# One core of a decoder layer: a gated mixer computed with tokens on the partitions instead of channels

## The chip, the cores and the metric

The kernel runs on one core of a Trainium2 chip. The time is that of one execution on the device, in microseconds. A core has five engines that run side by side, each working through its own list of instructions in order: TensorE (PE, with its weight loads shown apart as PEld), VectorE (DVE), ScalarE (ACT), GpSimd (POOL) and SyncE (SP), which starts transfers. They wait for one another by semaphores. TensorE's clock has two levels, 1.2 and 2.4 GHz.

## The reference

A layer takes 1088 tokens (1024 of a prompt and 8 x 8 of samples) with 1024 channels. After an RMS norm one projection makes three parts of 512 columns. The first goes to an S5 state-space mixer. The other two, u and v, go to the chunk mixer, which this case is about:

```python
def chunk_mixer(uv, ln_g, ln_b, w_s, b_s):
    uv = jax.nn.gelu(uv)
    u = uv[..., :CM_WIDTH]                              # CM_WIDTH 512
    v = layernorm(uv[..., CM_WIDTH:], ln_g, ln_b)
    ...
    vc = vp.reshape(Bn, n_chunks, Lc, CM_HEADS, CM_HEAD_DIM)   # 8 heads of 64, chunks of 128
    w = jnp.where(mask[None], w_s[:, :Lc, :Lc], jnp.zeros((), w_s.dtype))
    mixed = jnp.einsum('hts,bcshd->bcthd', w, vc)
    mixed = mixed + jnp.transpose(b_s[:, :Lc])[None, None, :, :, None]
    out = u * mixed
    return out, v[:, start:]

mix = jnp.concatenate([rmsnorm(o_s5, g_s5[l]), rmsnorm(o_cm, g_cm[l])], axis=-1)
x = x + mix @ w_out[l]
```

Behind it a gated feed-forward block (FFN) and a last norm follow.

## The kernel before

**Numbers.** A product of 32-bit numbers is made of three faster ones: each operand is split into a high and a low part (`split`: ScalarE copies the high part, L146, VectorE subtracts it, L147), and `mm3` issues three matmuls (L150 to L152). Small products (the spatial mixes, S5's own, transposes) are done on unsplit 32-bit operands; the trace shows such a matmul as two records, except for transposes.

**Layout.** xh and xl hold the split activations, features on the partitions: eight blocks of 128 features by 1088 tokens. The tokens stand in three pieces c of 384, 384 and 320 columns, or in nine tiles j of 128 (tile 8 takes the last 128 columns, of which the upper 64 are the samples). v is kept with tokens on the partitions, 128 x 9 x 512.

**Order.** One list of Python code is given to a scheduler, which simulates the engines and writes each engine's instructions in the order that comes out; `tc.issue_after` holds work back to a chosen point. PSUM banks are taken in turn from tags: mm has four, s5 three, sp one.

**Stages.** First the norm and the S5 part of the projection (pu, to us, through memory to U). From 72 us on two things run side by side:
- the S5 chain, eight times s5_a, s5_b, s5_c: four transposes (ptr, L502) of PT (VectorE, L491 to L493, from the transfer bc), matmuls sb (L509), kb (L517), yb (L585, L586), with many steps on VectorE between; its outputs ys go to memory as ys_d, and come back as g.
- the chunk mixer. `v_quarter` makes v (pv, 24 matmuls of N=256 a tile, tokens stationary, then a gelu on ScalarE, L650); `ln` normalizes it (a pow on GpSimd, L657). `cm_out(q, c)`, for q = 4 and 5 (the halves of u) and three pieces c, makes u with features on the partitions (`fm_group`, pu, 48 matmuls of N=384 or 320), scales it on VectorE by rB (the norm's factor, L673) and applies the gelu; then the spatial mix spt (L680): v is the weight, 64 columns for one head, w moves with 128 columns, two heads fill the two column halves of the array. VectorE adds the bias bB and multiplies by u (L691, L692). ScalarE squares, VectorE adds the squares up (sqo, L698). bB contains the row sums of w, which two matmuls rsw (L636) against a matrix of ones make early. `cm_mix(c)` sums the squares over partitions (ss, a matmul with ones, L164), makes the inverse root (`rsqrt_bc`, L171 to L174), scales on VectorE (L718) and splits into rows 4 to 7 of xh and xl.

Then s5_act splits g (L770, L771) into rows 0 to 3 of xh and xl, `glu` runs the pg matmuls (banks of tags mm and s5 in turn), `wo_tile` the output projection po, and the FFN follows.

Of the kernel before, what the change touches and what calls it, by code (L numbers as in the profile page):

```python
# [83 lines left out]
def layer_kernel(ctx: ExitStack, tc: tile.TileContext, A, O, dbg=None):  # L84
# [69 lines left out]
    SQB = {"cw": 1, "prep": SQP}  # L154
# [49 lines left out]
    cwp = Arena("cw", cwf, {"ur": (0, 384, 2), "sq": (768, 384, 1), "rsy": (1152, 384, 1)})  # L204
# [428 lines left out]
    for q in range(2):  # L633
        p = bank("rsw", "sp")
        with tc.issue_after(MM[RG].ins):
            PE.matmul(p, ones, wT[:, 4 * q:4 * q + 4, :].rearrange("p h t -> p (h t)"), start=True, stop=True)  # L636
        for i in range(4):
            m, h = divmod(4 * q + i, 2)
            hs = slice(64 * h, 64 * h + 64)
            V.scalar_tensor_tensor(bB[hs, m, :], p[hs, 128 * i:128 * i + 128], gcol("lnb", m)[hs], bB[hs, m, :],  # L640
                                   op0=ALU.mult, op1=ALU.add)
# [18 lines left out]
    def om_blocks(m, c):  # L660

        if c < 2:
            return [(v[:, 3 * c:3 * c + 3, 128 * m:128 * m + 128], 0, 384)]
        return [(v[:, 6:8, 128 * m:128 * m + 128], 0, 256), (v[:, 8, 128 * m:128 * m + 64], 256, 64)]

    def cm_out(q, c):

        n0, n = CH[c]
        pp = fm_group(q, c)
        for i in range(2):  # L670
            m = 2 * (q - 4) + i
            ur = cwp.tile([128, 384], F32, tag="ur", name="ur", bufs=2)[:, :n]
            V.tensor_tensor(ur, pp[i], rB[:, n0:n0 + n], ALU.mult)  # L673
            S.activation(ur, ur, AF.Gelu_apprx_tanh)
            p = bank("spt", "s5" if (q, c) > (5, 1) else "sp")[:, :n]
            for x in range(0, n, 128):
                j = (n0 + x) // 128
                r0, w = (0, wT) if j < 8 else (64, bd)
                for h in range(2):
                    PE.matmul(p[64 * h:64 * h + 64, x:x + 128 - r0], v[r0:128, j, 128 * m + 64 * h:128 * m + 64 * h + 64],  # L680
                              w[r0:128, 2 * m + h, :], start=True, stop=True)
            for om, o, w in om_blocks(m, c):
                d = [x[:, o:o + w] for x in (p, ur, sqo[:, n0:n0 + n])]
                t_ = 128 if w > 64 else 8
                d = [x.rearrange("p (j t) -> p j t", t=t_) for x in d]
                om = om.rearrange("p (j t) -> p j t", t=t_) if w == 64 else om
                if w > 64:
                    bias = bB[:, m:m + 1, :].to_broadcast([128, w // 128, 128])
                else:
                    bias = bB[:, m, 0:128:16].unsqueeze(2).to_broadcast([128, 8, 8])  # L690
                V.scalar_tensor_tensor(om, d[0], gcol("lng", m), bias, op0=ALU.mult, op1=ALU.add)  # L691
                V.tensor_tensor(om, om, d[1], ALU.mult)  # L692
                if m == 0:
                    S.activation(d[2], om, AF.Square)
                    continue
                sq = tmp_sq(cwp, w, "sq").rearrange("p (j t) -> p j t", t=t_)
                S.activation(sq, om, AF.Square)
                V.tensor_tensor(d[2], d[2], sq, ALU.add)  # L698
# [18 lines left out]
    def scaled_split(src, g, rb, hi, lo):
        V.scalar_tensor_tensor(src, src, g, rb, op0=ALU.mult, op1=ALU.mult)  # L718
        split(src, hi, lo)

    def cm_mix(c):
        n0, n = CH[c]
        rb = rsqrt_bc(cwp, sum_sq(sqo[:, n0:n0 + n], n), n, 1.0 / W)
        for m in range(4):
            for om, o, w in om_blocks(m, c):
# [614 lines left out]
```

## Time and profile before

| | before |
|---|---|
| median of 3 runs | 1105.35 us (1104.3 to 1107.51) |
| the profiled execution, its span | 1104.05 us, 1102.3 us |
| TensorE busy | 1049.9 us, 95% |
| VectorE busy | 852.9 us, 77% |
| ScalarE busy | 434.3 us, 39% |
| GpSimd busy | 320.5 us, 29% |
| mean granted clock of TensorE | .985 of full |

The busy shares are means over the whole span. What a change in one stage is worth is read in that stage, from what is busy and what waits there. The records of a matmul overlap: a matmul of .28 us whose successor starts .12 us later costs .12.

### The profile page before, as it was taken

What the parts mean: (1) busy time and instruction counts of PE and PEld (TensorE: products, weight loads), DVE (VectorE), ACT (ScalarE), POOL (GpSimd) and SP (SyncE); (2) the same over time, 40 slices, a digit from 0 to 9 for tenths busy, and PEclk for the clock granted to TensorE, in tenths of its full rate; (3) what the DMA queues carried; (4) which work ended last, traced back from release to release, by engine and by line L of the source; (5) the groups of instructions that cost most, each with busy time, mean ns of one, the idle gap of its engine ahead of it and who ended that gap; (6) DMA issues with size and microseconds to landing.
All of it is one profiled execution on the core that took longest, in us unless ns stands there. A gap on an engine that the chain in (4) does not pass through costs nothing.

```text
span 1102.3 us, 20323 instructions
## 1 busy us (share of the span) xinstructions
PE 1049.9 (95%) x7966; PEld 1026.8 (93%) x7966; DVE 852.9 (77%) x1724; ACT 434.3 (39%) x812; POOL 320.5 (29%) x287
## 2 busy tenths in 40 slices
PE   7899999979999799999999999999998999999994
PEld 6899998879999699999999999999998999999994
DVE  6987999999998996666666666657668768758886
ACT  7314333487544543233233232233244325314651
POOL 5010350000000435425435334435433333223220
PEclk9989999989999899999999999999999999999998
DMA  8342334375332113223224223133156816514304
GB/s 278 108 129 65 89 99 124 90 225 164 113 113 95 39 58 129 77 90 129 75 76 137 82 77 128 59 110 127 61 181 219 303 40 205 184 35 151 119 16 162
DMA packets 81520, 131.19 MB, mean 119 GB/s; under 512 B 8977, under 2 KB 60049, under 8 KB 81297
## 3 DMA queue, kind: packets, MB, share of 16 engines
q1 hardware_dynamic: 81424, 129.91, 36.3%
q8 instruction: 62, 1.02, 0.4%
q14 instruction: 34, 0.27, 0.1%
HBM read 90.43 MB, written 34.24 MB: 113 GB/s over the span
## 4 chain that ended last, share of the span: by engine, by line
PE 50%; DVE 7%; DMA 5%; issue 2%; ACT 1%; POOL 0%; DVEq 0%; ACTq 0%; POOLq 0%; SPq 0%
PE u L152 12%; PE u L150 12%; PE u L151 12%; DMA h<-hid_d 4%; PE ua L152 3%; PE ua L151 2%; PE ua L150 2%; PE ub L151 1%; PE ub L152 1%; DVE xl L147 1%; PE ub L150 1%; ACT xh L146 1%; DVE fb L147 1%; PE uc L151 1%; PE uc L152 1%
## 5 line engine op out<-in xcount | busy, mean ns | idle before, releaser
L1059 POOL TENSOR_TENSOR tS<-q,q 128x512 f32<-128x512 f32 x22 | 28.6, 1301 | 251.7 <-DVE h L921 146.1
L150 PE MATMUL u<-xh,h 128*128 128x272 f32 x344 | 99.1, 288 | 0.0
L151 PE MATMUL u<-xl,h 128*128 128x272 f32 x344 | 99.0, 288 | 0.0
L152 PE MATMUL u<-xh,h 128*128 128x272 f32 x344 | 98.9, 288 | 0.0
L146 ACT ACTIVATE h<-q 128x512 fp32r<-128x512 f32 (+1 forms) x83 | 50.7, 614 | 81.7 <-PE u L151 56.8
L147 DVE TENSOR_TENSOR h<-q,h 128x512 fp32r<-128x512 f32 (+1 forms) x83 | 72.6, 876 | 4.3 <-ACT h L146 2.5
L150 PE MATMUL pu<-xh,cwr 128*128 128x384 f32 (+1 forms) x192 | 65.5, 345 | 6.2 <-DVE us L303 6.2
L1097 ACT ACTIVATE st<-st 128x272 f32<-128x272 f32 x88 | 37.8, 431 | 72.0 <-DVE st L1119 34.8
L152 PE MATMUL pu<-xh,cwr 128*128 128x384 f32 (+1 forms) x192 | 65.1, 342 | 0.0
L151 PEld LDWEIGHTS u<-xl,h 128*128 128x128 f32 x344 | 64.9, 189 | 0.0
L151 PE MATMUL pu<-xl,cwr 128*128 128x384 f32 (+1 forms) x192 | 64.8, 338 | 0.0
L150 PEld LDWEIGHTS u<-xh,h 128*128 128x128 f32 x344 | 64.7, 188 | 0.0
L152 PEld LDWEIGHTS u<-xh,h 128*128 128x128 f32 x344 | 64.6, 188 | 0.0
L1064 POOL TENSOR_TENSOR tS<-tS,q 128x512 f32<-128x512 f32 x22 | 30.0, 1363 | 111.3 <-DVE h L147 59.6
L146 ACT ACTIVATE fb<-q 128x512 fp32r<-128x512 f32 (+1 forms) x64 | 38.9, 609 | 58.3 <-PE u L151 35.8
L152 PE MATMUL u<-xh,fb 128*128 128x272 f32 x208 | 61.1, 294 | 0.6 <-DVE fb L147 0.6
L150 PE MATMUL u<-xh,fb 128*128 128x272 f32 x208 | 60.6, 291 | 0.1
L151 PE MATMUL u<-xl,fb 128*128 128x272 f32 x208 | 60.5, 291 | 0.0
L147 DVE TENSOR_TENSOR fb<-q,fb 128x512 fp32r<-128x512 f32 (+1 forms) x63 | 53.4, 850 | 5.3 <-ACT fb L146 4.4
L152 PE MATMUL po<-xh,cwr 128*128 128x272 f32 x192 | 55.9, 291 | 0.0
L151 PE MATMUL po<-xl,cwr 128*128 128x272 f32 x192 | 55.8, 290 | 0.0
L150 PE MATMUL po<-xh,cwr 128*128 128x272 f32 x192 | 55.5, 289 | 0.0
(498 smaller groups left out, 4122.8 us busy)
## 6 DMA issues: line engine op xcount, KB each, us to landing
hid_d<-st SPq DMA_DIRECT2D x22, 952.0 KB, 4.2
h<-hid_d SPq DMA_DIRECT2D x28, 544.0 KB, 4.0
q<-in_w_gate_dram SPq DMA_DIRECT2D x22, 512.0 KB, 3.5
q<-in_w_up_dram SPq DMA_DIRECT2D x22, 512.0 KB, 3.5
q<-in_w_d_dram SPq DMA_DIRECT2D x16, 512.0 KB, 3.7
wo<-in_w_out_dram SPq DMA_DIRECT2D x14, 512.0 KB, 4.9
wi<-in_w_in_dram SPq DMA_DIRECT2D x12, 512.0 KB, 5.1
h<-hid_d SPq DMA_DIRECT2D x14, 408.0 KB, 3.1
```

The source lines that it names most:

```text
L146: S.activation(hi, src, AF.Copy)
L147: return (eng or V).tensor_tensor(lo, src, hi.bitcast(F32), ALU.subtract)
L150: PE.matmul(p, wh, ah, start=start, stop=False, **kw)
L151: PE.matmul(p, wh, al, start=False, stop=False, **kw)
L152: return PE.matmul(p, wl, ah, start=False, stop=stop, **kw)
L1059: P.tensor_tensor(tS, a21, a22, ALU.add)
L1064: P.tensor_tensor(tS, tS, a11, ALU.subtract)
L1097: S.activation(dst, src, AF.Silu)
```

## The change

u is now computed with tokens on the partitions, like v: `cm_u(q, j)` issues 24 matmuls of N=256 for a tile, and ScalarE applies the norm's factor (r1c, a column) and the gelu at once. The spatial mix takes w (128 x 128) as the weight and moves 64 columns of v for each of four heads, `cm_out(q, j)`. The bias becomes two tables BT of 128 x 512, made by 16 operations of ScalarE from 16 small matmuls rsw of N=1. VectorE adds and multiplies, 256 wide; ScalarE squares and sums along the row at once (ssc). `cm_mix(j)` works tile by tile: three tiny operations on GpSimd make the factor, ScalarE scales the row, TensorE transposes four blocks into one bank (pt), and for each of them ScalarE writes the high part and VectorE the low part. The three ss sums, rsqrt_bc's and the adding up of squares go, and ln's factor lng is applied within ln. `CL` sets how many tiles cm_out and cm_mix follow cm_u by.

```diff
+CL = 1, 3
-    cwp = Arena("cw", cwf, {"ur": (0, 384, 2), "sq": (768, 384, 1), "rsy": (1152, 384, 1)})
+    cwp = Arena("cw", cwf, {"ur": (0, 256, 2), "bt": (512, 512, 2)})
...
-    for i in range(2):
-        Q.dma_start(bB[64 * i:64 * i + 64], A["bB"][i:i + 1].to_broadcast([64, 4, 128]))
+    Q.dma_start(bsc, A["bB"])
...
-    for q in range(2):
-        p = bank("rsw", "sp")
-        with tc.issue_after(MM[RG].ins):
-            PE.matmul(p, ones, wT[:, 4 * q:4 * q + 4, :].rearrange("p h t -> p (h t)"), start=True, stop=True)
...
+    p = bank("rsw", "sp")
+    with tc.issue_after(MM[RG].ins):
+        for h in range(8):
+            PE.matmul(p[:, h:h + 1], wT[:, h, :], ones[:, 0:1], start=True, stop=True)
+            PE.matmul(p[64:128, 8 + h:9 + h], bd[64:128, h, :], ones[64:128, 0:1], start=True, stop=True)
+    S.activation(rsc[:, 0:8], p[:, 0:8], AF.Copy)
+    S.activation(rsc[64:128, 8:16], p[64:128, 8:16], AF.Copy)
+    BT = []
+    for i in range(2):
+        t, r0 = cwp.tile([128, W], F32, "bt"), 64 * i
+        for h in range(8):
+            hs, i_ = slice(64 * h, 64 * h + 64), 8 * i + h
+            S.activation(t[r0:128, hs], lnb[r0:128, hs], AF.Identity, scale=rsc[r0:128, i_:i_ + 1],
+                         bias=bsc[r0:128, i_:i_ + 1])
+        BT.append(t)
...
-        V.tensor_scalar(mv[:, j, 1:2], mv[:, j, 1:2], EPS, None, op0=ALU.add)
+        P.tensor_scalar(mv[:, j, 1:2], mv[:, j, 1:2], EPS, None, op0=ALU.add)
         P.tensor_tensor(mv[:, j, 1:2], mv[:, j, 1:2], mhalf[:, 0:1], ALU.pow)
-        V.tensor_scalar(vj, vj, mv[:, j, 0:1], mv[:, j, 1:2], op0=ALU.subtract, op1=ALU.mult)
+        V.scalar_tensor_tensor(vj, vj, mv[:, j, 0:1], lng, op0=ALU.subtract, op1=ALU.mult)
+        S.activation(vj, vj, AF.Copy, scale=mv[:, j, 1:2])
+    def cm_u(q, j):
+        p = bank("pv")
+        for k in range(8):
+            wh, wl = wq(q, k, slice(0, 256))
+            LAST["u"] = mm3(p[:, 0:256], xh[:, k, tok(j)], xl[:, k, tok(j)], wh, wl, k == 0, k == 7)
+        UR[q, j] = cwp.tile([128, 256], F32, "ur")
+        S.activation(UR[q, j], p[:, 0:256], AF.Gelu_apprx_tanh, scale=r1c[:, j:j + 1])
+    def cm_out(q, j):
+        ur = UR[q, j]
+        r0, w, b = (0, wT, BT[0]) if j < 8 else (64, bd, BT[1])
+        f0 = 256 * (q - 4)
+        p = bank("spt", ("sp", "mm")[j % 2])
+        for h in range(4):
+            PE.matmul(p[r0:128, 64 * h:64 * h + 64], w[r0:128, 4 * (q - 4) + h, :],
+                      v[r0:128, j, f0 + 64 * h:f0 + 64 * h + 64], start=True, stop=True)
+        om = v[r0:128, j, f0:f0 + 256]
+        V.tensor_tensor(om, p[r0:128, 0:256], b[r0:128, f0:f0 + 256], ALU.add)
+        V.tensor_tensor(om, om, ur[r0:128], ALU.mult)
+        S.activation(ur[r0:128], om, AF.Square, accum_out=ssc[r0:128, j, q - 4:q - 3])
+    def cm_mix(j):
+        r0 = 0 if j < 8 else 64
+        rc = ssc[r0:128, j, 0:1]
+        P.tensor_tensor(rc, rc, ssc[r0:128, j, 1:2], ALU.add)
+        P.tensor_scalar(rc, rc, 1.0 / W, EPS, op0=ALU.mult, op1=ALU.add)
+        P.tensor_tensor(rc, rc, mhalf[r0:128, 0:1], ALU.pow)
+        S.activation(v[r0:128, j, :], v[r0:128, j, :], AF.Copy, scale=rc)
+        p = bank("pt")
+        for m in range(4):
+            PE.transpose(p[:, 128 * m:128 * m + 128], v[:, j, 128 * m:128 * m + 128], idn)
+        for m in range(4):
+            src = p[:, 128 * m + r0:128 * m + 128]
+            hi, lo = (x[:, 4 + m, 128 * j:128 * j + 128 - r0] for x in (xh, xl))
+            S.activation(hi, src, AF.Copy, scale=gcol("gcm", m))
+            V.scalar_tensor_tensor(lo, src, gcol("gcm", m), hi.bitcast(F32), op0=ALU.mult, op1=ALU.subtract)
...
-    for c in range(3):
-        cm_out(4, c)
+    def cm_run(q):
+        for j in range(9 + CL[q - 4]):
+            if j < 9:
+                cm_u(q, j)
+            with tc.issue_after(LAST["u"].ins):
+                if 0 <= j - CL[0] < 9:
+                    cm_out(q, j - CL[0])
+                if q == 5 and 0 <= j - CL[1] < 9:
+                    cm_mix(j - CL[1])
+    cm_run(4)
     load_wq(5)
...
-    for c in range(3):
-        cm_out(5, c)
-        if c:
-            cm_mix(c - 1)
-    cm_mix(2)
+    cm_run(5)
```

Three places of the engines' orders follow; lines of the changed kernel are shifted by one and more. The first is TensorE at the beginning of the chunk mixer. Before, from the end of the last S5 projection (pu) to the first transposes of S5 (ptr), with 134 pv rows between the first rsw and ptr:

```order
L152 MATMUL pu_568<-xh,cwr 128x320
L636 MATMUL rsw<-wT,ones 128x512
L150 MATMUL pv<-cwr,xh 128x256
...
L152 MATMUL pv<-cwr,xl 128x256
L502 MATMUL ptr<-idn,PT 128x128 x4
L150 MATMUL pv<-cwr,xh 128x256
```

And in the changed kernel, where the two kinds of rsw alternate eight times and 92 pv rows stand before ptr:

```order
L153 MATMUL pu_568<-xh,cwr 128x320
L636 MATMUL rsw<-ones,wT 128x1
L637 MATMUL rsw<-ones,bd 64x1
...
L151 MATMUL pv<-cwr,xh 128x256
...
L152 MATMUL pv<-cwr,xh 128x256
L503 MATMUL ptr<-idn,PT 128x128 x4
L153 MATMUL pv<-cwr,xl 128x256
```

The first ptr has moved ahead of 42 pv matmuls. The second place is TensorE's end of the chunk mixer, before: the last S5 product yb, the last sum and mixes, and the first pg of the next stage.

```order
L586 MATMUL yb<-Hp,QK 128x136
L164 MATMUL ss<-sqo,ones 128x384
L680 MATMUL spt<-wT,v 64x128 x4
L680 MATMUL spt<-bd,v 64x64 x2
L150 MATMUL pg<-xh,wgh 128x384 x7
L151 MATMUL pg<-xl,wgh 128x384
L152 MATMUL pg<-xh,wgl 128x384
```

In the changed kernel 58 rows of u (tile name pv), three mixes and two tiles' transposes stand between the last yb and the first pg; then pg matmuls alternate with the last tiles. This is the piece from the end of u(5,8), the last tile of u, on:

```order
L153 MATMUL pv<-cwr,xl 128x256
L686 MATMUL spt<-v,wT 128x64 x4
L703 MATMUL pt<-idn,v 128x128 x4
L686 MATMUL spt<-v,bd 64x64 x4
L151 MATMUL pg<-xh,wgh 128x384
...
L153 MATMUL pg<-xh,wgl 128x384
L703 MATMUL pt<-idn,v 128x128 x12
L151 MATMUL pg<-xh,wgh 128x384
L152 MATMUL pg<-xl,wgh 128x384
```

The spt are the mixes of tiles 7 and 8, the pt between them the transposes of tile 5, the twelve transposes those of tiles 6, 7 and 8, and 13 pg stand before them. The third place is GpSimd at the same time (L697 adds the two halves' sums, L698 scales, L699 is the pow; 128x1 is tile 7, 64x1 tile 8). Before, GpSimd has nothing of the mixer here.

```order
L697 TENSOR_TENSOR ssc_1637<-ssc_1637 128x1
L698 TENSOR_SCALAR ssc_1637<-ssc_1637 128x1
L697 TENSOR_TENSOR ssc_1637<-ssc_1637 64x1
L699 TENSOR_TENSOR ssc_1637<-ssc_1637,mhalf_95 128x1
L698 TENSOR_SCALAR ssc_1637<-ssc_1637 64x1
L699 TENSOR_TENSOR ssc_1637<-ssc_1637,mhalf_95 64x1
```

The pow of tile 7 stands behind the first operation of tile 8, which reads the square sums of tile 8.

## Rows read from the trace of the kernel before

**Rows 1.** Windows: length, busy PE, PEld, DVE, ACT, POOL (instructions), clock, DMA share, GB/s.

```profile
72.00:225.00 153.00, 151.21 (x1161) 139.78 (x1159) 141.09 (x320) 59.05 (x134) 27.98 (x29) 1.00 0.37 103
225.00:231.00 6.00, 0.09 (x4) 0.00 (x0) 6.00 (x13) 5.96 (x11) 0.00 (x0) 0.81 1.09 303
231.00:247.00 16.00, 15.90 (x79) 15.90 (x80) 15.16 (x33) 13.86 (x31) 0.00 (x0) 0.86 0.72 245
247.00:357.00 110.00, 110.00 (x848) 108.91 (x846) 99.66 (x231) 58.48 (x111) 0.00 (x0) 1.00 0.37 124
```

**Rows 2.** Timeline, 223 to 232: start, length, instruction, idle time before it.

```profile
223.63 0.40 ACT L587 ACTIVATE ys<-yb 128x272 f32<-128x272 f32 x1 [0.29 <-PE yb L586]
224.51 4.10 SPq L757 DMA_DIRECT2D g<-ys_d  x4
224.76 0.33 PE L680 MATMUL spt<-bd,v 64*64 64x64 f32 x4
230.53 1.23 ACT L770 ACTIVATE xh<-g 128x384 fp32r<-128x384 f32 x3
231.10 2.61 PE L150 MATMUL pg<-xh,wgh 128*128 128x384 f32 x7 [6.01 <-ACT xh L770]
```

**Rows 3.** Timelines of VectorE and TensorE before the first ptr.

```profile
85.65 0.69 DVE L491 TENSOR_TENSOR PT<-bc,wr 128x512 f32<-128x512 f32 x1 [3.34 <-DMA bc<-in_bc_dram]
...
89.20 0.68 DVE L493 TENSOR_TENSOR PT<-PT,ptt 128x512 f32<-128x512 f32 x1
...
85.56 0.28 PE L151 MATMUL pv<-cwr,xh 128*128 128x256 f32 x1
...
90.00 0.28 PE L152 MATMUL pv<-cwr,xl 128*128 128x256 f32 x1
90.12 0.60 PE L502 MATMUL ptr<-idn,PT 128*128 128x128 f32 x4
...
90.67 0.28 PE L151 MATMUL pv<-cwr,xh 128*128 128x256 f32 x1
```

**Rows 4.** Timeline of TensorE, two runs of pu without gaps.

```profile
142.52 0.33 PE L151 MATMUL pu<-xl,cwr 128*128 128x384 f32 x1
...
144.60 0.34 PE L151 MATMUL pu<-xl,cwr 128*128 128x384 f32 x1
...
167.60 0.31 PE L150 MATMUL pu<-xh,cwr 128*128 128x320 f32 x1
...
169.94 0.31 PE L151 MATMUL pu<-xl,cwr 128*128 128x320 f32 x1
```

**Rows 5.** Timeline of TensorE around one group of sb and one of spt.

```profile
117.56 0.28 PE L150 MATMUL pv<-cwr,xh 128*128 128x256 f32 x1
117.68 1.09 PE L509 MATMUL sb<-U,Pg 128*128 128x136 f32 x8
...
118.73 0.28 PE L152 MATMUL pv<-cwr,xl 128*128 128x256 f32 x1
...
164.58 0.34 PE L152 MATMUL pu<-xh,cwr 128*128 128x384 f32 x1
164.84 0.88 PE L680 MATMUL spt<-wT,v 128*64 128x128 f32 x12
...
165.90 0.31 PE L151 MATMUL pu<-xl,cwr 128*128 128x320 f32 x1
```

**Rows 6.** Groups by line and shape, 72 to 225: busy us, mean ns.

```profile
L509 PEld LDWEIGHTS sb<-U,Pg 128*128 128x128 f32 x64 | 8.1, 190 | 0.5 <-ACT cwf L674 0.4
...
L680 PEld LDWEIGHTS spt<-wT,v 128*64 128x64 f32 x128 | 6.9, 136 | 3.3 <-issue 1.4 <-PE yb L586 0.5 <-DVE v L691 0.3
```

**Rows 7.** GpSimd's pow (ns: least, median, most), a split, an operation of 256 columns.

```profile
L657 POOL TENSOR_TENSOR mv<-mv,mhalf x9: 541/1512/3400, 117.6 to 151.4; 128x1 f32<-128x1 f32 x9
...
L147 DVE TENSOR_TENSOR cwr<-wi,cwr 128x1024 fp32r<-128x1024 f32 x7 | 8.5, 1214 | 0.5 <-ACT cwr L146 0.4
...
226.69 0.41 DVE L698 TENSOR_TENSOR sqo<-sqo,cwf 128x256 f32<-128x256 f32 x1
```

More of the change, by code (lines that the diff above doesn't have):

```diff
@@ L152, in mm3 @@
         return PE.matmul(p, wl, ah, start=False, stop=stop, **kw)
-    SQB = {"cw": 1, "prep": SQP}
+    SQB = {"prep": SQP}
     def tmp_sq(pl, n, name):
@@ L601, in layer_kernel @@
         return
-    lgb = lncp.tile([128, 2 * W + 64], F32, tag="L", name="lgb")
+    lgb = lncp.tile([128, 2 * W], F32, name="lgb")
     lng, lnb = lgb[:, 0:W], lgb[:, W:2 * W]
-    bB = lncp.tile([128, 4, 128], F32, name="bB")
+    bsc = lncp.tile([128, 16], F32, name="bsc")
+    rsc = lncp.tile([128, 16], F32, name="rsc")
     bd = lncp.tile([128, 8, 64], F32, name="bd")
@@ L615, in layer_kernel @@
     Q.dma_start(lnb, A["ln"][1:2, :].to_broadcast([128, W]))
-    for i in range(2):
-        Q.dma_start(bB[64 * i:64 * i + 64], A["bB"][i:i + 1].to_broadcast([64, 4, 128]))
+    Q.dma_start(bsc, A["bB"])
     def tok(j):
         return slice(128 * j, 128 * j + 128) if j < 8 else slice(NT - 128, NT)
-    jk = tmp_sq(cwp, 128, "jk")
+    jk = cwp.tile([128, 128], F32, "ur")
     for j in range(9):
         V.scalar_tensor_tensor(jk, rB[:, tok(j)], 1.0, idn, op0=ALU.mult, op1=ALU.mult, accum_out=r1c[:, j:j + 1])
-    sqo = lncp.tile([128, NT], F32, tag="L", name="sqo")
     wT = lncp.tile([128, 8, 128], F32, name="wT")
@@ L631, in layer_kernel @@
     V.copy_predicated(wT, mk[:, 0:128].unsqueeze(1).to_broadcast([128, 8, 128]), r)
-    for q in range(2):
-        p = bank("rsw", "sp")
-        with tc.issue_after(MM[RG].ins):
-            PE.matmul(p, ones, wT[:, 4 * q:4 * q + 4, :].rearrange("p h t -> p (h t)"), start=True, stop=True)
[L637 to L641, printed above, removed]
+    p = bank("rsw", "sp")
[13 more added lines that the diff above has]
+        BT.append(t)
     st = lncp.tile([128, 9, 6], F32, name="st")
     mv = lncp.tile([128, 9, 2], F32, name="mv")
+    ssc = lncp.tile([128, 9, 2], F32, name="ssc")
     def v_quarter(q, j):
@@ L655, in ln @@
         V.bn_aggr(mv[:, j, :], st[:, j, :])
-        V.tensor_scalar(mv[:, j, 1:2], mv[:, j, 1:2], EPS, None, op0=ALU.add)
+        P.tensor_scalar(mv[:, j, 1:2], mv[:, j, 1:2], EPS, None, op0=ALU.add)
         P.tensor_tensor(mv[:, j, 1:2], mv[:, j, 1:2], mhalf[:, 0:1], ALU.pow)
-        V.tensor_scalar(vj, vj, mv[:, j, 0:1], mv[:, j, 1:2], op0=ALU.subtract, op1=ALU.mult)
[L660 to L698, printed above, removed]
@@ new lines, in ln @@
+        V.scalar_tensor_tensor(vj, vj, mv[:, j, 0:1], lng, op0=ALU.subtract, op1=ALU.mult)
+        S.activation(vj, vj, AF.Copy, scale=mv[:, j, 1:2])
+    UR = {}
+    def cm_u(q, j):
[5 more added lines that the diff above has]
+        S.activation(UR[q, j], p[:, 0:256], AF.Gelu_apprx_tanh, scale=r1c[:, j:j + 1])
@@ L709, in layer_kernel @@
         t = raw(o, (W,))
-        P.tensor_tensor(t, v[:, j, :], lng, ALU.mult)
-        P.tensor_tensor(t, t, lnb, ALU.add)
+        P.tensor_tensor(t, v[:, j, :], lnb, ALU.add)
         Q.dma_start(O[o], t[r0:128])
-    for c in range(3):
-        cm_out(4, c)
-    load_wq(5)
[L717 to L725, printed above, removed]
-                d = [rb[:, o:o + w]] + [x[:, 4 + m, n0 + o:n0 + o + w] for x in (xh, xl)]
-                if w > 64:
-                    d = [x.rearrange("p (j t) -> p j t", t=128) for x in d]
-                scaled_split(om, gcol("gcm", m), *d)
-    for c in range(3):
-        cm_out(5, c)
-        if c:
-            cm_mix(c - 1)
-    cm_mix(2)
+    def cm_run(q):
[8 more added lines that the diff above has]
+    cm_run(4)
+    load_wq(5)
+    cm_run(5)
     s5w_st.close()
@@ L1305, in lay @@
     A["mk"] = mk
-    A["bB"] = bs[:, CP].reshape(4, 2, 128).transpose(1, 0, 2)
+    A["bB"] = np.concatenate([bs[:, CP], bs[:, np.concatenate([tt, tt])]]).T
     return {k: np.ascontiguousarray(x) for k, x in A.items()}
```

## The prediction

> **What bounds the kernel now.** I read the windows first. Between 72 and 225 us, where the chunk mixer and the S5 chain run, TensorE is busy 151.2 of 153.0 us at full clock, VectorE 141.1, ScalarE 59.1, GpSimd 28.0 [rows 1]. So TensorE's work there is time one for one; what VectorE saves there is worth nothing while TensorE stays full. Then come six microseconds with TensorE all but idle, then sixteen in which its granted clock is .86 of full on average (part of them at 1.2 GHz), then again a stretch without a gap [rows 1]. The timeline of 223 to 231 us explains the six: the last gelu of S5 starts at 223.63, its output goes through memory (ys_d out, g back, issued from 224.51), ScalarE's first split of g starts at 230.53, and the first pg at 231.10 waits for that split [rows 2]. TensorE has nothing else: its last spt starts at 224.76.
>
> **The cost of one matmul** is the distance of starts in a run without gaps. N=256 (pv): 85.56 to 90.00 is 37 steps, .120 us [rows 3]. N=384 (pu): 2.08/12 = .173; N=320: 2.34/16 = .146 [rows 4]. A small group is priced as start of the second matmul behind it, less start of the last ahead of it, less the two pitches: four transposes .67 - .24 = .43 [rows 3]; twelve spt records 1.32 - .173 - .146 = 1.00; eight records of sb, with weights of 128 columns, 1.17 - .24 = .93 [rows 5].
>
> **1. u token by token.** Before: 192 matmuls of N=384 and 96 of N=320: 33.3 + 14.0 = 47.3 us. After: 18 tiles of 24 with N=256: 432 x .120 = 51.8. **+4.5.** The operands are those of pv, so there is little to bound: +-.5.
>
> **2. The mixes.** Before there are twelve groups of twelve records (of N=128, or eight of these and four of N=64), two heads side by side on column halves of the array: 12 x 1.00, and a little more where a group is split in two: 12.6. After: 18 groups of four heads, each head two records, w as the 128-column weight, 64 columns moving. No row shows that. The nearest is sb: also eight records, also 128-column weights, but 136 moving columns, .93. If the moving columns set the pace, a record costs 64/136 of .116, a group .44. If the weight load does, then by the loads' durations, 190 ns for 128 columns and 136 for 64 [rows 6], a column takes .84 ns, 128 take .108 and the group .86, with its start and end about .93. I take .93, since 64 moving columns give a load half the time that it needs to hide: 18 x .93 = 16.7. **+4.1.** Ends: .44 gives -4.7; .93 and .35 on top for an emptied array (1.00 of an spt group less 6 x .109, the pace of such records, .116 x 128/136) gives +10.4.
> The form given up is the one that the Trainium skill, page TensorEngine Tiling (Array Packing), section When to Use Tiling, asks for: with 64 moving columns, swap stationary and streaming and tile the columns in two. Its section Key Properties adds that a change of tiling mode drains the engine, which the .35 bears out. By that rule alone, doubled streaming of 12 x .65 = 7.8 us, the mixes would cost 15.7 against 12.6, +3.1, and the sum would be 1 us lower.
>
> **3. Transposes back.** Nine groups of four, each .43. **+3.9.**
>
> **4. Column sums of squares.** Three ss matmuls against ones go, since Square now sums along the free axis. Each is two records of N=384 (one of 320): at sb's pace per column .65, .65, .55. **-1.8.**
>
> **5. The start.** The first ptr can't come earlier than now: it waits for PT, whose last operation runs 89.20 to 89.88 on VectorE, behind an operation at 85.65 that waited 3.34 us for the bc transfer [rows 3]. VectorE's order up to it is unchanged from that transfer on. Between the first rsw and that ptr TensorE has 134 pv matmuls before and 92 after (the order rows of the beginning). The 42 that are now behind it, 42 x .120, must be paid later: **+5.0**. The 32 records of the 16 small rsw (16 loads of 128 columns, 16 of 64: 16 x .108 + 16 x .054 = 2.6, against 4 records of 512 columns, 1.7 at sb's pace per column) lie within that wait and add nothing. If the wait weren't there, they alone would count: +.9, the lower end.
>
> Work: 4.5 + 4.1 + 3.9 - 1.8 + 5.0 = **+15.7**.
>
> **6. The wait for g.** After the last yb the changed order has 58 pv, three spt groups and two of transposes before the first pg: 58 x .12 + 3 x .93 + 2 x .43 = 10.6 us of work that doesn't need S5. The path from ys (223.63) to the split (230.53) is 7 us. So the wait goes, **-6.0**, and with it the slow clock behind it: 79 instructions took 16.0 us, at .173 they take 13.7 [rows 1]: **-2.3**.
>
> **7. What is late next.** The cover has to come from somewhere: u(5,7), u(5,8) and their mixes now stand among the pg, and the last tile's chain is exposed. Let T be the start of u(5,8). TensorE then has 24 pv (2.9), spt (.93), pt of tile 5 (.43), spt of tile 8 (.9), 13 pg (2.25), pt of tile 6 (.43): 7.8 us. Behind that stand pt of 7, pt of 8 and 108 pg, the first of which needs a PSUM bank of the mm tag, the oldest of which is tile 5's pt. Tile 8's chain: u ends at T + 3; spt(7) and spt(8) at T + 4 to 5; on VectorE come four operations of 256 columns (.41) with two weight splits of 1.21 among them [rows 7]: T + 8; Square on ScalarE, .4: T + 8.5. GpSimd computes the factor in three tiny operations, and the pow of tile 7 stands behind the first of tile 8 (the order rows of GpSimd), so both tiles wait for Square(8). A pow takes 1.51 us in the median [rows 7]: tile 7 at T + 10.4, scaled on ScalarE (.5) T + 11, its transposes; tile 8 T + 12.3 and T + 13. Then the four copies and four subtractions per tile, on ScalarE and VectorE, which free tile 5's bank last, about 1.5 more: T + 14.5. TensorE has run out at T + 7.8 and does .9 us of transposes meanwhile: **+6** idle (0 if the banks come free before it runs out; 10 if each pow takes some 3 us and ScalarE stands behind the split of wo, which waits for a transfer). A slow clock behind it could cost 2 again; not in the sum.
>
> Hidden: gelu, Square, Identity and Copy on ScalarE (59 of 153 us busy), the added small operations on GpSimd, the VectorE work (fewer operations in all). If that cover goes, it is rival B.
>
> Sum: 15.7 - 8.3 + 6 = +13.4, against the profiled execution's 1104.05: **1117.4**, call it 1117. The median of the runs shown is 1105.35, so a per cent's tenth lies in that alone; 0.3%, 3.3 us, is what a measurement can tell from no change: 1102.0 to 1108.7 is "same".
>
> **The rivals.**
> Forecast, 52%: one wait replaced by another, with more work: 1112 to 1122.
> A, 18%: the new wait is hidden. Then 1111.4. For it: the 108 pg need only one free bank to go on. Against: the chain of step 7 is serial through four engines, and in the sixteen microseconds that it falls into VectorE is busy 15.2 and ScalarE 13.9 [rows 1], with work that stays.
> B, 20%: ScalarE, VectorE and GpSimd, now in one chain per tile (factor, scaling, transposes, four pairs of copy and subtraction), starve TensorE at several tiles. A tile of q=5 gives TensorE 24 x .12 + .93 + .43 = 4.2 us; the chain's copies come to about 3, but a pow reaches 3.4 us when VectorE is busy [rows 7]. With one such stall of 1 us for each of the nine tiles: 1126.
> C, other side, 10%: narrow mixes are nearly free. In the 18 groups the loads run ahead under the streams of u, so that the 64 moving columns set the pace: .44 each, -8.8. With the wait of step 7 it gives 1108.6, without it 1102.6; it decides from 1102 down, when a group costs under .41 and the last tile is hidden, since 1111.4 - 18 x (.93 - .41) = 1102.0. At .3 it is 1100. For it: pv's pitch of .120 shows loads of 128 columns hidden beside 256 columns. Against: sb.
> The Trainium skill, page TensorE: Matmul & The Clock Gate, in its table of gaps between matmuls, gives some 25 ns for up to 64 columns; a group would then be .2 and the total 1104.2 with the wait, 1098.2 without. No row here shows such a pace.
>
> **How the numbers follow.** The likeliest is 1117. Below: A, and C with the wait (1108.6). Above: B. Leaving out C's fast end and the worst of B, the range is 1104 to 1127. Faster by over 0.3%: C with the last tile hidden, and nothing else, .07. Same: the rest of C and the lower edge of A with cheaper mixes or a smaller step 5, .11. Slower: .82.
>
> **What would show it.** pv pitch .12 in u; a group of four spt at .9 (or .45); TensorE waiting at the first ptr for PT until about 90; no wait of the first pg for g; instead, some 260 us in, a wait of pt or pg for ScalarE or VectorE of about 6 us. I am wrong if that wait is missing (A), if waits of 1 us stand at every tile (B), if a group of mixes is under .5 (C), or if bc arrives several microseconds earlier.

## The result, and the profile after

| | before | after |
|---|---|---|
| median of the runs | 1104.82 us (1104.11 to 1107.51, 4 runs) | 1123.62 us (1121.95 to 1124.16, 4 runs) |
| ratio, 95% interval | | 1.016 (1.0145 to 1.0176) |
| span of the profiled execution | 1102.3 us | 1121.9 us |
| TensorE, VectorE, ScalarE, GpSimd busy | 1049.9, 852.9, 434.3, 320.5 us | 1069.5, 834.5, 451.1, 335.6 us |

The change is slower by 1.6%, 18.8 us by the medians. TensorE is busy for 19.6 us more, VectorE for 18.4 less. First the windows of the changed kernel, which answer to [rows 1] (columns as there):

```profile
72.00:76.00 4.00, 4.00 (x34) 3.77 (x32) 4.00 (x9) 1.06 (x1) 0.00 (x0) 1.00 0.83 210
76.00:82.00 6.00, 6.00 (x39) 5.99 (x39) 1.90 (x6) 5.78 (x18) 0.00 (x0) 0.72 1.03 342
82.00:90.00 8.00, 8.00 (x70) 8.00 (x69) 6.68 (x12) 3.74 (x11) 0.00 (x0) 1.00 0.09 30
...
90.00:225.00 135.00, 132.34 (x1098) 127.46 (x1097) 114.53 (x254) 62.76 (x155) 33.91 (x46) 1.00 0.36 97
...
231.00:245.00 14.00, 14.00 (x111) 13.73 (x110) 10.70 (x30) 12.20 (x33) 2.36 (x6) 1.00 0.26 100
245.00:260.00 15.00, 10.06 (x41) 9.00 (x40) 9.71 (x25) 11.67 (x31) 3.92 (x6) 0.66 0.87 281
260.00:274.00 14.00, 14.00 (x88) 13.73 (x87) 8.51 (x21) 10.00 (x23) 0.00 (x0) 1.00 0.52 161
```

Two stretches stand out: 76 to 82 us with the clock at .72, though TensorE shows no gap, and 245 to 260, where TensorE is busy 10.1 of 15 us and the clock is .66. The six idle microseconds at 225 are gone. TensorE's chain of waits between 72 and 400 us, its first rows and one further down:

```profile
PE pt L703 <- ACT v L700: 4.2, 2, 3.4
PE ss L165 <- DVE fbt L907: 1.9, 1, 1.9
...
PE yb L586 <- DMA mb<-mb: 1.1, 1, 1.1
...
PE pg L151 <- DVE xl L708: 0.7, 1, 0.7
```

pt and the pg behind it now wait where pg waited for g. TensorE's timeline from u(5,8), the last tile of u, on (its first matmul at 237.94):

```profile
236.62 0.28 PE L153 MATMUL pv<-cwr,xl 128*128 128x256 f32 x1
236.74 1.00 PE L686 MATMUL spt<-v,wT 128*128 128x64 f32 x8
237.57 0.61 PE L703 MATMUL pt<-idn,v 128*128 128x128 f32 x4
237.94 0.36 PE L151 MATMUL pv<-cwr,xh 128*128 128x256 f32 x1
...
245.26 0.60 PE L703 MATMUL pt<-idn,v 128*128 128x128 f32 x4
249.28 1.11 PE L703 MATMUL pt<-idn,v 128*128 128x128 f32 x4 [3.42 <-ACT v L700]
251.21 1.11 PE L703 MATMUL pt<-idn,v 128*128 128x128 f32 x4 [0.81 <-ACT v L700]
253.03 0.69 PE L151 MATMUL pg<-xh,wgh 128*128 128x384 f32 x1 [0.71 <-DVE xl L708]
253.51 0.52 PE L152 MATMUL pg<-xl,wgh 128*128 128x384 f32 x1
253.83 0.52 PE L153 MATMUL pg<-xh,wgl 128*128 128x384 f32 x1
```

TensorE is out of work 7.8 us after u(5,8) has begun, tile 7 can be transposed at 11.3, tile 8 at 13.3, and pg goes on at 15.1. From 253 us pg runs at .32 us a matmul, at 1.2 GHz (the granted clock is .50 from 249 to 257 us), where [rows 4] have .173.

To see where the time went, each TensorE instruction is given the time from its start to the next one's start, less idle time, and these are summed by tile from the first rsw to the first po (185.8 us before, 201.4 after):

| | before | after | difference |
|---|---|---|---|
| matmuls of v and u (pv, pu) | 54.19 + 51.10 | 110.28 | +5.0 |
| mixes (spt) | 10.74 | 14.58 | +3.8 |
| transposes back (pt) | | 5.41 | +5.4 |
| rsw | .91 | 4.01 | +3.1 |
| column sums (ss) | 1.84 | .35 | -1.5 |
| pg | 26.25 | 26.64 | +.4 |
| idle before pg | 6.01 | .71 | -5.3 |
| idle before pt | | 4.23 | +4.2 |
| other idle time, S5's matmuls | | | +.5 |
| sum | | | **+15.7** |

After that the feed-forward entry gives 2 us back (the first u starts 15.5 us later, the 309th 13.3 later), and its last part, ua to uc, takes 5 more. Start times of the first form of ua before, then after (minimum, median and maximum duration, first and last start):

```profile
L150 PE MATMUL ua<-xh,h x90: 284/289/391, 836.6 to 1077.3; 128*128 128x272 f32 x90
```

```profile
L151 PE MATMUL ua<-xh,h x90: 283/289/428, 851.1 to 1096.9; 128*128 128x272 f32 x90
```

14.5 us at the first, 19.6 at the last. The order of TensorE's last 5,300 rows, which hold this part, is the same in both kernels.

### The profile page after: what moved, and what is told of

The parts are those of the page before. It is cut to its first block, busy times and chain, and to the rows that moved or that the text cites. A ratio compares the mean times of both kernels' runs of the same rounds, so it can differ in the third digit from the quotient of the medians.

```text
span 1121.9 us, 20798 instructions
## 1 busy us (share of the span) xinstructions
PE 1069.5 (95%) x8168; PEld 1049.2 (94%) x8168; DVE 834.5 (74%) x1682; ACT 451.1 (40%) x884; POOL 335.6 (30%) x321
## 4 chain that ended last, share of the span: by engine, by line
PE 55%; DVE 8%; DMA 8%; POOL 3%; ACT 3%; issue 3%; SPq 0%; DVEq 0%; POOLq 0%; ACTq 0%
PE u L152 11%; PE u L153 11%; PE u L151 11%; DMA h<-hid_d 4%; PE po L151 3%; PE po L152 3%; PE po L153 3%; PE ua L153 2%; PE ua L151 2%; PE ua L152 2%; DMA hid_d<-st 1%; PE ub L152 1%; PE ub L153 1%; PE ub L151 1%; DVE xl L148 1%
## 5 line engine op out<-in xcount | busy, mean ns | idle before, releaser
L151 PE MATMUL pv<-cwr,xh 128*128 128x256 f32 x288 | 83.4, 292 | 0.6 <-ACT cwr L147 0.4
L153 PE MATMUL pv<-cwr,xl 128*128 128x256 f32 x288 | 83.0, 289 | 0.0
L152 PE MATMUL pv<-cwr,xh 128*128 128x256 f32 x288 | 82.8, 288 | 0.0
L151 PEld LDWEIGHTS pv<-cwr,xh 128*128 128x128 f32 x288 | 55.5, 194 | 1.3 <-ACT cwr L147 0.7
L151 PE MATMUL po<-xh,cwr 128*128 128x272 f32 x192 | 56.5, 295 | 0.0
L152 PEld LDWEIGHTS pv<-cwr,xh 128*128 128x128 f32 x288 | 55.7, 194 | 0.6 <-issue 0.6
```

What stands on the lines that cost most here:

```text
L151: PE.matmul(p, wh, ah, start=start, stop=False, **kw)
L152: PE.matmul(p, wh, al, start=False, stop=False, **kw)
L153: return PE.matmul(p, wl, ah, start=False, stop=stop, **kw)
```

## The experiments

Times of one comparison stand beside runs of the kernel before on the same chip, whose median lay between 1107.3 and 1109.1; so ratios are compared. Every length from the first rsw to the first po below is read as in the table above.

**1. The last tiles' mixing behind the first glu piece (late_mix).**

```diff
-                if q == 5 and 0 <= j - CL[1] < 9:
+                if q == 5 and 0 <= j - CL[1] < 6:
                     cm_mix(j - CL[1])
...
     for c in range(3):
         glu(c)
+        if c == 0:
+            with tc.issue_after(LAST["pg"].ins):
+                for j in range(6, 9):
+                    cm_mix(j)
```

> The changed kernel (1123.6 us) with the last three tiles' scaling and transposes held back until the 48 matmuls of the first glu piece are issued. Theory 1, the chain of the last tiles leaves TensorE without work: 36 more pg stand ahead of the transposes, the wait of pt for ScalarE (3.4 + 0.8 + 0.7 us) and the slow clock behind it (some 2.4 us) go, 1114 to 1116. Rival, the wait is one for PSUM banks or for VectorE's and ScalarE's total work and only moves: 1121 to 1124, with a wait of pg or po of some 5 us in its place.

Ratio 1.0114 (1.0092 to 1.0136), median 1119.96 beside 1107.3; 197.1 us from rsw to po, 4.4 less. Its window and the waits from 225 to 275 us:

```profile
245.00:260.00 15.00, 13.20 (x81) 11.99 (x80) 11.99 (x24) 14.04 (x33) 3.95 (x6) 1.00 0.66 204
```

```profile
PE pt L704 <- ACT sg L785: 1.0, 2, 0.7
PE ss L166 <- DVE acc L188: 0.6, 1, 0.6
PE pg L152 <- ACT sg L785: 0.2, 1, 0.2
```

The wait shrinks from 4.9 to 1.9 us and the clock stays at full: pg costs 25.0 us in place of 26.6, pt 4.3 in place of 5.4. Theory 1 stands; the gain, 5 us by the ratios, is smaller than expected (1114 to 1116 would be 8 to 10 us less), since 1.9 us of waiting is left and TensorE loses 1.7 ahead of it (rsw, yb, u), as in the second trace of the unchanged kernel (experiment 7).

**2. The output weights behind the last tile (late_wo).** `LAST["mix"]` is the last subtraction of cm_mix.

```diff
-    with tc.issue_after(g5_ld.ins), tc.issue_after(SPL["v"].ins), tc.issue_after(SPL["s"].ins):
+    with tc.issue_after(g5_ld.ins), tc.issue_after(SPL["v"].ins), tc.issue_after(SPL["s"].ins), tc.issue_after(LAST["mix"].ins):
         for q in range(2):
             load_wo(1, q, q)
```

(and the same for the other two quarters)

> The changed kernel with only the loading and splitting of the output weights held back until the last tile is mixed; TensorE's order is the same. Theory 1, the three copies of 1.05 us on ScalarE and the three subtractions of 1.22 us on VectorE stand in the last tiles' chain: the idle time ahead of the last transposes falls by 2.5 to 3.5 us, 1120 to 1121, if the weights come in time for the output projection. Rival, the chain is long for GpSimd's three operations and the pairs of copy and subtraction: less than 1 us, 1123. A third outcome, the weights come late: slower than 1124, with a wait of po for them.

Ratio 1.0121 (1.0098 to 1.0144); 199.6 us from rsw to po. The wait of pt falls from 4.2 to 2.6 us, that of pg from .7 to .2, and TensorE's order up to po is the same as in the changed kernel. So the splits of the output weights were a part of the chain, 2.2 us of it where theory 1 expected 2.5 to 3.5, and what is left is the tiles' own. No wait of po came of it. Of the 4 us between the ratios, 1.9 lie ahead of po; the last part of the feed-forward, which varies, is 2.6 us shorter here (experiment 7). In the changed kernel ScalarE's timeline shows the copies of these splits in the chain:

```profile
241.16 1.99 ACT L147 ACTIVATE cwr<-wo 128x1024 fp32r<-128x1024 f32 x2
243.06 0.46 ACT L677 ACTIVATE cwf<-pv,r1c 128x256 f32<-128x256 f32 x1
243.42 1.05 ACT L147 ACTIVATE cwr<-wo 128x1024 fp32r<-128x1024 f32 x1
244.36 0.71 ACT L700 ACTIVATE v<-v,ssc 128x512 f32<-128x512 f32 x1
```

u(5,8) ended at about 240.9; its gelu (L677) begins at 243.06, behind two weight copies.

**3. Both delays (late_both).** The edits of 1 and 2 together.

> The changed kernel with both delays together (the last three tiles' mixing behind the first glu piece, the output weights behind that). Theory 1, tail gains add up as far as there is wait left (1.9 us after the first alone): 1 to 2 us below the first alone, some 1.009 of before. Rival, the output weights now come too late, since their loading waits for a mix that stands behind pg: a wait of po for them, and slower than either.

Ratio 1.0098 (1.0074 to 1.0123); 197.0 us from rsw to po. No wait of pt over .1 us is left, one of pg of .8, and po waits for nothing, so the rival fails. Theory 1's gain over the first alone is not shown: up to po it is the same (197.0 and 197.1 us; 1.0 us more of waiting before yb takes the place of what pt no longer waits), and the ratios' intervals overlap. With most of the tail's price gone the kernel is still slower than before by 1%: 11.2 us from rsw to po.

**4. Row sums from wide matmuls (wide_rsw).**

```diff
-        for h in range(8):
-            PE.matmul(p[:, h:h + 1], wT[:, h, :], ones[:, 0:1], start=True, stop=True)
-            PE.matmul(p[64:128, 8 + h:9 + h], bd[64:128, h, :], ones[64:128, 0:1], start=True, stop=True)
-    S.activation(rsc[:, 0:8], p[:, 0:8], AF.Copy)
...
+                PE.matmul(p, ones, wT[:, 4 * i:4 * i + 4, :].rearrange("p h t -> p (h t)"), start=True, stop=True)
...
+                V.scalar_tensor_tensor(jk, p[:, 128 * h:128 * h + 128], 1.0, idn, op0=ALU.mult, op1=ALU.mult,
+                                       accum_out=rsc[:, 4 * i + h:4 * i + h + 1])
```

> The changed kernel with the row sums of w from three wide matmuls against ones (512 columns) and 16 VectorE operations that pick the diagonal, in place of 32 records of one column. Theory 1, these records cost TensorE's time (4.0 us of it) and the clock behind them: 3 wide ones are 1.3 to 2 us, the granted clock stays at full from 76 to 82 us, in all 2 to 4 us less, 1119.5 to 1121.5. Rival, the prediction's step 5, the first transposes of S5 wait for bc anyway: the time saved turns into a wait there, 1123 to 1124.

Ratio 1.0141 (1.012 to 1.0161), some 2 us less. Its windows:

```profile
76.00:82.00 6.00, 6.00 (x47) 5.52 (x46) 4.74 (x21) 1.75 (x7) 0.00 (x0) 1.00 1.03 304
82.00:90.00 8.00, 6.53 (x48) 5.59 (x47) 5.49 (x12) 4.98 (x12) 0.00 (x0) 1.00 0.26 94
```

The clock is full where it was .72. rsw costs 1.9 in place of 4.0 us, pv and u 108.7 in place of 110.3. So the one-column matmuls cost 3.7 us of TensorE's time between these two traces, 1.6 of it by the slow clock behind them. In the five other traces that have them (those of experiments 1, 2, 3, 6 and 7) rsw, pv and u together take 1.0 to 1.3 us more still, with a longer slow stretch. Most of what is saved comes back as waits: 1.5 us of rsw for VectorE, 1.3 more of pg, 1.2 more of yb; from rsw to po it is 200.7 us, .8 less than the changed kernel. The scheduler also laid out the tail anew. So theory 1 holds for TensorE's time and the clock, but a gain in the kernel's time is not shown, as the ratio's interval overlaps that of the changed kernel. The rival had the idea right, that the time turns into waits, and the place wrong: ptr waits for nothing.

**5. More TensorE work in the kernel before (padded_before).**

```diff
-        for k in range(8):
+        for k in 2 * list(range(8)) if q == 3 and j < 5 else range(8):
```

> The kernel before, with 120 of the 432 pv matmuls issued twice (a sum restarted, so the result is the same): 14.4 us more TensorE work at 72 to 225 us and nothing else. Theory 1, TensorE's work there is time one for one: 1104.8 + 14.4 = 1119.2, and the wait for g stays. On the late loss (some 4 us in the last part of the feed-forward, where the instruction order of both kernels is the same): if it comes from a shift in time alone, it shows here too, and the time is 1122 to 1124; if it belongs to the change, the offset stays at 14.4. Rival, the S5 chain hides part of it: under 1115.

Ratio 1.0092 (1.0059 to 1.0125), median 1117.5 beside 1107.3, single runs from 1113.3 to 1121.4. From rsw to po 190.2 us, only 4.5 more. Theory 1 fails: 10 us and not 14.4 are lost, and the wait for g does not stay. The rival has the direction, but not the place: the windows show no gap and a full clock where the wait for g was.

```profile
72.00:225.00 153.00, 153.00 (x1180) 144.21 (x1179) 136.59 (x305) 56.58 (x129) 20.83 (x29) 1.00 0.42 116
225.00:240.00 15.00, 15.00 (x119) 13.06 (x118) 14.24 (x32) 11.95 (x24) 0.00 (x0) 1.00 0.55 182
```

TensorE's added work pushed u's last pieces behind the last yb, where they fill the wait: of 14.4 us, 6 and the slow clock behind come back. pg, now at full clock, takes 24.6 us in place of 26.3. In po then 3.0 us are lost to a wait for VectorE and some 2 more. The last part of the feed-forward starts 11.3 us later than before's and takes 251.5 us, within what before's own two traces take (249.3 and 251.8): in this trace a shift in time alone does not bring the late loss.

**6. Wider mixes (wide_moving).**

```diff
-            PE.matmul(p[r0:128, 64 * h:64 * h + 64], w[r0:128, 4 * (q - 4) + h, :],
-                      v[r0:128, j, f0 + 64 * h:f0 + 64 * h + 64], start=True, stop=True)
+            n_ = 128 if h < 3 else 64
+            PE.matmul(p[r0:128, 64 * h:64 * h + n_], w[r0:128, 4 * (q - 4) + h, :],
+                      v[r0:128, j, f0 + 64 * h:f0 + 64 * h + n_], start=True, stop=True)
```

> The changed kernel, with three of four matmuls of each mix moving 128 columns in place of 64 (the next head's 64 columns go along and are written over by the next matmul; the result is the same). Theory 1, the load of the 128-column weight sets the pace, .11 us a record: nothing changes, a group still .9. Rival, the moving columns set it: six of eight records take twice as long, .6 us a group and some 11 us in all.

A single run, 1122.82 us. One of its groups on TensorE's timeline:

```profile
238.04 1.00 PE L687 MATMUL spt<-v,wT 128*128 128x128 f32 x8
238.87 0.39 PE L704 MATMUL pt<-idn,v 128*128 128x128 f32 x2
```

.83 us from the group to the next instruction, as with 64 columns (236.74 to 237.57). So theory 1 holds: the moving columns don't set the pace there. That it is the weight, and not some cost that every record has, is borne out by tile 8, whose weight bd has 64 rows and 64 columns. Its group in the changed kernel, and here with 128 columns moving:

```profile
242.26 0.68 PE L686 MATMUL spt<-v,bd 64*64 64x64 f32 x8
242.87 0.44 PE L151 MATMUL pg<-xh,wgh 128*128 128x384 f32 x1
```

```profile
243.56 0.98 PE L687 MATMUL spt<-v,bd 64*64 64x128 f32 x8
244.47 0.45 PE L151 MATMUL pg<-xh,wgh 128*128 128x384 f32 x1
```

.61 us with the narrow weight, less than .83, and .91 with twice the columns: under a 64-column weight the moving columns do count. Over all, spt takes 15.5 in place of 14.6 us, some .6 of it in the two groups of tile 8. In the other groups the weights' loads set the pace.

**7. The two kernels again (before_again, after_again).**

> The kernel before, unchanged, for a second trace of it. Theory 1 on the late loss of some 4 us in the last part of the feed-forward: it hangs on how that part's transfers happen to fall and not on the change; this trace shows losses against the first one of 1 us or more there, and its time lies over 1105. Rival, it is the change's: the two traces of before agree within 0.5 us in each stretch.

> The changed kernel, unchanged, for a second trace. Theory 1: from 72 us to the start of the output projection it takes the same time as the first trace within 0.5 us (201.4 us from the first rsw), the last part of the feed-forward differs by 1 us or more. Rival: that part again takes 5 us longer than before's, as in the first trace.

Single runs on this chip: 1110.55 and 1127.91 us. From rsw to po: 186.7 and 202.4 us, against 185.8 and 201.4 of the first traces, so this part repeats within 1 us (the .5 that was expected is missed). The last part does not: from the first to the last matmul of ua it took 249.3 and 251.8 us in the two traces of before, 254.5 and 257.2 in those of the changed kernel. Over the fourteen traces of this study, seven kernels with before's mixer (those of part 8 among them) lie from 248.9 to 251.8 us, seven with the tile-wise mixer from 251.8 to 257.2. So neither theory holds whole: this part varies by 2.5 us between two executions of one kernel, and is still some 4 us longer behind the change (means 250.6 and 254.4). In it TensorE waits for high parts that ScalarE makes late, since ScalarE itself waits for gated rows from memory (in the changed kernel's first trace two waits of 1.8 and 2.0 us, at 862 and 885 us). There, behind these waits, TensorE's clock falls:

```profile
862.60:866.00 3.40, 3.40 (x16) 3.19 (x15) 3.40 (x7) 0.69 (x2) 0.07 (x1) 0.50 1.00 360
886.50:889.90 3.40, 3.36 (x16) 3.32 (x15) 3.40 (x6) 1.37 (x2) 2.62 (x2) 0.51 1.02 417
```

Six of the seven traces with the tile-wise mixer have such stretches at 1.2 GHz in this part, 3.4 to 10.2 us in all; the seventh, late_wo, has none and took 251.8 us, and none of the seven with before's mixer has any. By an estimate from these rows (half of the time at 1.2 GHz is lost) the slow clock makes 2.4 us of the 3.8 between the means; TensorE's idle time, 8.7 us on the mean in place of 7.5, makes another 1.1. Which of the change's effects lengthens the waits and lets the clock fall there stays open.

**8. Attempts to fill the wait for g without the change.** cover_before holds the last piece of u back; half_cover its last 24 matmuls; pool_before moves additions and subtractions of the mixer to GpSimd; pool_cover does both.

```diff
+        with tc.issue_after(LAST["yb"].ins) if c == 2 else ExitStack():
-        cm_out(5, c)
+            cm_out(5, c)
```

```diff
+            with tc.issue_after(LAST["yb"].ins) if (q, c, m) == (5, 2, 1) else ExitStack():
                 MM[q, c] = mm3(pp[m], wh, wl, xh[:, k, n0:n0 + n], xl[:, k, n0:n0 + n], k == 0, k == 7)
```

```diff
-                V.tensor_tensor(d[2], d[2], sq, ALU.add)
+                P.tensor_tensor(d[2], d[2], sq, ALU.add)
...
-        split(src, hi, lo)
+        split(src, hi, lo, P)
```

> The kernel before, with one thing moved: the last piece of u (48 matmuls of N=320, 7.0 us) and its mixes are held back until the last S5 product yb is issued, so that TensorE has work while g comes back from memory. Theory 1, the 6.0 us wait for g and the slow clock behind it (2.3 us) are the whole price of that place: 1096 to 1098. Rival, VectorE (15.2 of 16 us busy there) gets the last piece's operations on top and is late with the splits of g and of the output weights: the wait moves to pg or po, 1102 to 1106.

> The kernel before, with the last 24 matmuls of u (N=320, 3.5 us) and their mixes held back until the last yb, half of what the covered version moved. Theory 1, TensorE's work ahead of the last yb is what hides the S5 chain, and each microsecond moved behind it shows as a wait of yb: the wait for g falls by some 4 us, waits of yb rise by 2 to 4, no change within 3 us. Rival, the chain has some slack, and only the whole piece was too much: 3 to 5 us faster than before.

> The kernel before, with the adding of squares (12 operations of .2 to .55 us) and the subtractions that make the low parts in the mixer's last step (16 of .2 to .55 us) on GpSimd in place of VectorE, some 11 us of VectorE's work. Theory 1, VectorE's work is hidden behind TensorE and the wait for g is a transfer's: no change, 1104 to 1109 by the chip. Rival, the shared work of VectorE sets the end of S5: the last yb and with it g come earlier, up to 6 us less.

> Both: the last piece of u held back behind the last yb, and the same VectorE work on GpSimd. Theory 1, the covered version lost its gain because VectorE, which carries both S5 and the mixer, is late (4.8 us of waits of yb, 4.3 of ss): with 11 us less on VectorE the waits of ss go and part of those of yb, 4 to 6 us less than the covered version, about the kernel before or 2 us under it. Rival, yb waits for transfers (mb, gw): no better than 1110 to 1113.

Ratios: cover 1.0047 (1.0029 to 1.0066), half 1.0039 (1.0024 to 1.0054), GpSimd 1.0043 (1.0023 to 1.0062), GpSimd with cover 1.0106 (1.0084 to 1.0129). None beats the kernel before; all four are slower, by .4 to 1.1%. TensorE's waits from 72 to 262 us in the covered kernel:

```profile
PE ss L164 <- DVE cwf L172: 2.9, 1, 2.9
PE yb L585 <- DMA mb<-mb: 2.7, 2, 2.1
PE yb L586 <- DVE fs L579: 1.4, 2, 1.2
PE ss L164 <- DVE v L691: 1.3, 1, 1.3
```

The wait for g is gone and pg runs at full clock (24.3 us in place of 26.3), but yb waits 4.8 us in all and ss 4.3: the pu matmuls that were moved had hidden S5's own chain, and VectorE's work now ends last. The slow clock has only moved, to the place of these waits:

```profile
218.00:228.00 10.00, 6.75 (x23) 5.34 (x24) 6.86 (x14) 5.19 (x9) 0.00 (x0) 0.50 0.19 51
```

So theory 1 fails, and the rival is right that the wait moves, but not where to (neither pg nor po). The half cover shows the same in small: the wait for g falls from 6.0 to 2.1 us, yb, ss and sb wait 5.2 in place of 1.6, and from rsw to po it is 186.0 us, as before (185.8), which is theory 1 up to po. In pool_before GpSimd takes .93 us in the median for the addition (up to 3.46), VectorE .47; yb waits 3.8 us and nothing is gained, so its rival fails. With both edits ss still waits 4.1 us and yb 5.3: taking work off VectorE did not mend the covered version.

## Why the prediction was right, and where it was not

The direction and the main mechanism, one wait replaced by another and more work on TensorE, were right (forecast 1117, range 1104 to 1127, measured 1123.6). The measured time lies 1.6 us above the 1112 to 1122 given to that outcome, and the reason of step 5 was wrong. By its steps:

**1, u:** +4.5 forecast. pv and u together cost 110.3, of which 1.6 us is the slow clock at 76 to 82 (experiment 4); the rest, 108.7 - 105.3, is +3.4. The bound of .5 was too tight: before's pu took 51.1, not the 47.3 of the pitches alone. Nearly all of the 3.9 between them falls on matmuls that stand first or last in a run of pu, beside mixes and S5's products.

**2, the mixes:** +4.1 forecast, +3.8 measured, and the reason holds: the load of 128 columns sets the pace, not the moving columns (experiment 6). The two sides were both priced some 2 us too high (12.6 and 16.7, where the table has 10.7 and 14.6, as it leaves what a mix costs its neighbours with them); only the difference bears comparison. With it rival C falls. So does, for this case, the gap of some 25 ns: the table of the Trainium skill, page TensorE: Matmul & The Clock Gate, section Back-to-back issue gap, gives it for a single matmul without the load of a weight, as that section says, and here every matmul has a load; no record of the changed kernel's mixes took less than .055 us to the next. For the load the Trainium skill, page TensorE: Matmul & The Clock Gate, section LDWEIGHTS, gives the columns divided by 1.2 in ns, 107 for 128; the group's .83 to .84 over eight records is .10 to .11 each.

**3, the transposes:** +3.9 forecast, +5.4 measured; at full clock 4.0 (experiment 3), so the price of one was right, and the rest is the slow clock behind the wait of step 7.

**4, the column sums:** -1.8 forecast, -1.5.

**5, the start:** +5.0 forecast. The reason failed. "The first ptr can't come earlier than now" took the arrival of bc for fixed. It came 2.3 us earlier (VectorE's first PT operation; 3.5 earlier between the two second traces):

```profile
83.32 0.69 DVE L492 TENSOR_TENSOR PT<-bc,wr 128x512 f32<-128x512 f32 x1 [5.38 <-DMA bc<-in_bc_dram]
```

[Rows 3] have 85.65. SyncE's timeline shows a part of why: it issues bc behind a piece of weights, which waits for a buffer that VectorE's split frees. Before and after:

```profile
78.26 0.34 SPq L242 DMA_DIRECT2D wi<-in_w_in_dram  x1
...
79.67 0.43 SPq L485 DMA_DIRECT2D bc<-in_bc_dram  x1
```

```profile
75.36 0.34 SPq L243 DMA_DIRECT2D wi<-in_w_in_dram  x1
...
77.01 0.42 SPq L486 DMA_DIRECT2D bc<-in_bc_dram  x1
```

Before, four of the eight operations that made bB (.33 to .36 us each, 75.54 to 77.01) stood ahead of that split on VectorE. The change took them away, and the queue moved up by 1.5 us; the rest is an earlier start of the transfers ahead (us_d at 66.78 in place of 68.18), whose cause was not followed. The arrival also varies without the change: in the five kernels of experiments 5 and 8, which keep these operations, the first PT operation starts between 83.9 and 85.4. ptr then waited for nothing (it starts at 88.69, where PT was ready at 87.55); the price was rsw itself, 3.1 us (its 32 records took 4.0 us where 2.6 were reckoned, before's four .9 where 1.7 were), and 1.6 of slow clock behind it. The size, 4.7, is near the forecast by chance.

**6, the wait for g:** gone, as forecast (-6.0; the table's -5.3 has the new wait of pg, .7, in it). The -2.3 for the slow clock behind it was not saved, since another wait brought it back: pg took .4 more than before. It was also sized too high: at full clock pg takes 24.6 (experiment 5), 1.7 less than before.

**7, what is late next:** forecast +6, hand-worked to T + 14.5 for the first pg; measured T + 15.1. TensorE ran out at T + 7.8, as worked out. Of the 7.3 us up to 253.03 the two groups of transposes at full clock would take .9: 6.4 lost. The term left out is what was off: the slow clock behind the wait, which "could cost 2 again; not in the sum". It cost 1.4 in the transposes (5.4 - 4.0) and 1.7 in pg (26.6 - 25.0 in experiment 1). One link was blamed too much: tile 7's pow stood only .3 us behind tile 8's first operation (247.93 and 247.66 on GpSimd); and it took .55 us, not 1.51, while tile 7's addition took 1.24, so that the time of the chain came out nearly right over wrong parts. The weight splits, which the sum had between the products, were worth more (experiment 2).

So the forecast for po, +13.4, became +15.7, mainly by the clock: pg's +.4 in place of -2.3 is 2.7 us, u's -1.1 goes against it, and the other differences are under .6 each (with the transposes' 1.4 of slow clock counted to step 7, as above). The rest of the 19.6, the longer last part of the feed-forward, was in no term: 5.1 us in these two traces, by the estimate of experiment 7 3.4 of them from the slow clock there.

Rival A, the tail hidden, is what experiment 3 nearly built by hand; it is still slower than before, as A said. Rival B, a stall at each tile, did not come: pt waits at two tiles only.

## What to carry to other kernels

A stage in which TensorE has no gap is priced by starts: narrower moving operands, transposes and tiny matmuls are paid in full there, unless a later wait takes them up (in the padded kernel some 10 of 14.4 us, up to po). That 18 us less VectorE work buys nothing by itself there is argued, not shown, as no run took that work away alone; in the nearest, pool_before, 11 us less of it on VectorE gained nothing. Work that fills one wait is taken from in front of another: where a chain ends behind the moved work, its own latency shows (here both in the changed kernel's last tiles and in the covered kernel's yb), with a slow clock on top. A wait of two microseconds can so cost as much again in the clock, here also far behind the change, in the last part of the feed-forward. A transfer's arrival is not fixed as long as a queue ahead of it waits for a buffer that a changed engine frees.

## What the runs showed of the hardware

With the one-column matmuls the granted clock fell while TensorE counted as busy all the time. In the changed kernel's first trace they took 4.0 us (4.00 of 4.00 us busy from 72 to 76), and from 78 to 80 us the clock was .50, with TensorE busy 2.00 of 2.00:

```profile
78.00:80.00 2.00, 2.00 (x12) 2.00 (x11) 0.00 (x0) 1.99 (x7) 0.00 (x0) 0.50 1.09 332
```

From 74 to 84 us, always without a gap, the clock was .83 in this trace and .66 in the five others with one-column row sums; in all eight with wide ones (wide_rsw and the seven with before's mixer) it was 1.00. The changed kernel's second trace, then before's first:

```profile
74.00:84.00 10.00, 10.00 (x60) 9.85 (x61) 4.55 (x13) 6.38 (x23) 0.00 (x0) 0.66 0.89 269
74.00:84.00 10.00, 10.00 (x80) 9.52 (x80) 8.12 (x22) 0.48 (x1) 0.00 (x0) 1.00 0.99 287
```

And eight matmul records of a mix with a 128-column weight take .83 us whether 64 or 128 columns move, some .10 to .11 each; with tile 8's weight of 64 columns they take .61 and .91.
